# Seam order of weight splits and turned input, and weight halves in modulation steps, in a two-block transformer on one core

## The chip, the core and the metric

The kernel is one program on one NeuronCore of a Trainium2 chip. The metric is the device time of one execution in microseconds (us). Before the change three runs gave 1286.58, 1288.45 and 1289.17 us; their median is 1288.45 us. Engines are named as in the profile: PE is the matmul engine and PEld its weight load, DVE the vector engine, ACT the scalar engine, POOL the GpSimd engine, SP the engine whose queue issues the loads.

## The reference

Two blocks run one after the other on the same 256 tokens of width 1024, all in float32:

```
h = swiglu(rms_norm(x), ffn1_w_in, ffn1_w_out)          # 1024 -> 2 x 2816 -> 1024
x = x + 0.5 * rms_norm(h)
x = x + rms_norm(token_mixing(rms_norm(x)))              # retention + neighbourhood attention
x = x + 0.5 * rms_norm(swiglu(rms_norm(x), ffn2_w_in, ffn2_w_out))
mod = silu(c) @ ada_w + ada_b                            # 2 layers x 6 vectors of 1024
for i in (0, 1):                                         # moba attention, then differential attention
    shift1, scale1, gate1, shift2, scale2, gate2 = mod[i]
    y = attention_i(x * (1 + scale1) + shift1)
    x = layer_norm(sqrt(2) * x + (1 + gate1) * y)
    y = square(relu((x * (1 + scale2) + shift2) @ up)) @ down   # 1024 -> 4096 -> 1024
    x = layer_norm(sqrt(2) * x + (1 + gate2) * y)
```

What matters here is that 198 slots of 1 MB of weights and 48 MB of `ada_w` (the matrix of the modulation) are read once, and that each stage starts from a normalised, scaled and shifted copy of `x` with features on the partitions, which I call the turned input.

## The kernel before

The stages are, in order: ffn1, mixing, ffn2, attention 0, mlp 0, attention 1, mlp 1. A matmul in full float32 precision is made of three matmuls on operands of a reduced float32 type: a value `w` is split into a high part `wh` (rounded by a copy) and a low part `wl = w - wh`, and an input likewise; `mmA` and `mmB` issue high by high, high by low and low by high.

**The stream of weights.** `Stream` handles all weights in one fixed sequence of slots of 1 MB, each of two halves. A half is loaded to a `raw` tile (RAW = 6 of them, line 79 or 81, on SP's queue), ACT copies it to `wh` (line 115), and DVE subtracts to `wl` (line 93). One such step is `piece()`. The DVE part isn't issued at once: it goes to the list `late` and is issued by `flush(n)`, which leaves the newest `n` of the list. At most RING = 8 halves are held beyond the oldest one in use. Between the weights stand the halves of the modulation: a piece of `ada_w` is no weight but a multiply-add on DVE into `adacc` (line 339); after eight of them `ada_parts` (lines 345 to 358) cuts the sum into three bf16 parts by turns on ACT and DVE, and `spare` multiplies them by ones on PE (24 matmuls of one column, or three of 512 columns) when the next feed-forward step has room.

**What sets the order.** Every engine runs its instructions in the order in which this program issues them. PE's work is issued half by half, and after each half comes a `tick()`: it advances the stream (`Stream.tick`, line 135) by up to two pieces and then runs one turn of the background generators (the hidden activations, attention pairs, `ada_parts`). So what stands ahead of what on ACT and DVE is fixed by how many pieces a tick issues:

```
        for n in range(2):
            p = self.next_pos()
            if self.si >= len(self.seq) or p >= self.prog + look or 2 * p >= self.done + RING:
...
            mod = self.si not in self.wpos
            self.piece()
            if mod:
                break
```

`use(n, b)` (line 154) is called when PE's work for slot n is about to be issued; it makes the missing pieces and flushes the whole list.

**Seams.** A stage ends in `down_tail`: the four banks of the last product, by token half t and feature half f, are handed to `post.bank(t, f)`. `PostRms` (ffn1, mixing, ffn2) and `PostLn` (both attentions, mlp 0) normalise and add to `x`. Behind the last bank `ahead(3)` makes three pieces, and `flush(post.low)` keeps `low` splits back (2 for `PostRms`, 1 for `PostLn`). Then the next stage begins with `projT`: it calls `use` for its two slots and `turn(1)` for the second token half (the first was turned inside `down_tail`, by `mid`). `turn_of` (line 586) transposes eight 128 x 128 blocks on PE (tile `xt`). With a shift `c` given (the seams into attention and mlp) ACT scales and shifts them into `hf` (line 606), the high part goes to `XX` by a copy on ACT for t = 0 (line 612) and on DVE for t = 1 (line 610), and DVE subtracts the low part (line 613), in groups of 2, 2 and 4 blocks. Without a shift ACT writes the high part and DVE the low part straight from `xt` (lines 597, 598). PE's first matmul of the second half needs the first group.

Of the kernel before, what the change touches and what calls it, by code (L numbers as in the profile page):

```python
# [12 lines left out]
AF = mybir.ActivationFunctionType  # L13
# [35 lines left out]
class Stream:  # L49
# [39 lines left out]

    def flush(self, n=0):  # L90
        while len(self.late) > n:
            wl, raw, wh = self.late.popleft()
            self.nc.vector.tensor_tensor(wl, raw, wh.bitcast(F32), OP.subtract)  # L93

    def next_pos(self):
# [7 lines left out]
    def piece(self, lag=1):  # L103
        nc, i, h = self.nc, self.si, self.half
        raw = self.raw.pop((i, h))
        self.half += 1
        if self.half == 2:
            self.half, self.si = 0, i + 1
        if self.seq[i][0] == "w":
            n = self.wpos[i]  # L110
            assert 2 * n + h < self.done + RING, (n, h, self.done)
            wh = self.pool.tile([128, 1024], F32R, name="wh", bufs=RING)
            wl = self.pool.tile([128, 1024], F32R, name="wl", bufs=RING)
            self.parts[n, h] = (wh, wl)
            nc.scalar.activation(wh, raw, AF.Copy)  # L115
            self.late.append((wl, raw, wh))
            if lag is not None:
                self.flush(lag)
            self.load_to()
        else:  # L120
            self.flush()
            self.ada(self.seq[i][3], h, raw)
            self.load_to()
# [11 lines left out]
    def tick(self):  # L135
        self.prog += 0.5
        look = 1.5 if self.prog < 5 else LOOK
        for n in range(2):
            p = self.next_pos()
            if self.si >= len(self.seq) or p >= self.prog + look or 2 * p >= self.done + RING:  # L140
                if n == 0:
                    self.flush()
                    self.load_to()
                break
            mod = self.si not in self.wpos
            self.piece()
            if mod:
                break

    def ahead(self, n=1):  # L150
# [5 lines left out]
    def use(self, n, b):  # L156

        while self.next_pos() <= n + 0.5:
            self.piece()
        self.flush()  # L160
        return [[t.rearrange("p (k f) -> p k f", f=b) for t in self.parts[n, h]] for h in range(2)]

    def release(self, n, h):
# [8 lines left out]
def block_kernel(ctx, tc, A, out):  # L172
    nc = tc.nc
    V, SC, PE, GP = nc.vector, nc.scalar, nc.tensor, nc.gpsimd
# [14 lines left out]
    def w2(name, bufs=None):  # L189
        return work.tile([128, 512], F32, name=name, tag="w2", bufs=4)  # L190
# [135 lines left out]
    mod = const.tile([128, 96], F32, name="mod")  # L326
# [3 lines left out]
    def ada(key, h, w):  # L330
        l, s, i = key
        kb = 2 * i + h
        if kb == 0:
            ada_drain()
            adacc[0] = big.tile([128, D], F32, name="adacc")
            V.tensor_scalar(adacc[0], w, csil[:, 0:1], None, op0=OP.mult)
            return
        t = adacc[0]
        V.scalar_tensor_tensor(t, w, csil[:, kb:kb + 1], t, op0=OP.mult, op1=OP.add)  # L339
        if kb == 7:  # L340
            ada_now.append(ada_parts(l, s, t))
            start(ada_now[0], 1)
# [3 lines left out]
    def ada_parts(l, s, t):  # L346

        parts = [adap[-1].tile([128, D], BF16, name=f"ada{i}", bufs=1) for i in range(3)]
        SC.activation(parts[0], t, AF.Copy)
        yield 1  # L350
        V.tensor_tensor(t, t, parts[0], OP.subtract)
        yield 1
        SC.activation(parts[1], t, AF.Copy)
        yield 1
        V.tensor_tensor(parts[2], t, parts[1], OP.subtract)
        yield 1
        ada_now.clear()
        ada_out.append((l, s, parts, None if s in (2, 5) else 0))

# [92 lines left out]
    def proj(bank, then=nothing):  # L452

        n = nxt()
        for h, (wh, wl) in enumerate(st.use(n, 256)):
            for c in range(2):
                cs = slice(c * 128, (c + 1) * 128)
                for k in range(4):
                    mmB(two(bank)[:, c], wh[:, k, cs], wl[:, k, cs], XX[:, 4 * h + k],
                        h == 0 and c == 0 and k == 0, h == 1 and k == 3)  # L460
            st.release(n, h)
            if h:
                then()
            tick()

    def projv(bank, then=nothing):

        n = nxt()
        for h, (wh, wl) in enumerate(st.use(n, 256)):
            for t in range(2):  # L470
                for k in range(4):
                    mmA(two(bank)[:, t], wh[:, k], wl[:, k], XX[:, 4 * h + k, :, TS[t]],
                        h == 0 and t == 0 and k == 0, h == 1 and k == 3)
            st.release(n, h)
            if h:
                then()
            tick()

    def projA(banks, X, nk=KB, then=nothing):

        for i in range(nk // 4):
            n = nxt()
            for h, (wh, wl) in enumerate(st.use(n, 512)):
                for t in range(2):
                    for k in range(2):
                        kk = 4 * i + 2 * h + k
                        mmA(banks[t], wh[:, k], wl[:, k], X[:, kk, :, TS[t]], kk == 0, kk == nk - 1)
                st.release(n, h)
                if kk == nk - 1:
                    then()  # L490
                tick()
# [94 lines left out]
    def turn_of(src, a, c, alloc=gu):  # L586

        def turn(t):
            ps = [alloc("xt"), alloc("xt")]
            for k in range(8):  # L590
                PE.transpose(ps[k // 4][:, k % 4 * 128:k % 4 * 128 + 128], src[:, t, k * 128:(k + 1) * 128], ident)
            if c is None:
                for i in range(4):
                    for b in range(2):
                        k = 4 * b + i
                        x, h, l = ps[b][:, i * 128:(i + 1) * 128], XX[:, k, 0, TS[t]], XX[:, k, 1, TS[t]]
                        SC.activation(h, x, AF.Copy, scale=a[:, k:k + 1])
                        V.scalar_tensor_tensor(l, x, a[:, k:k + 1], h.bitcast(F32), op0=OP.mult, op1=OP.subtract)  # L598
                return
            for k0, n in ((0, 2), (2, 2), (4, 4)):  # L600
                if k0 != 2:
                    w = w2("hf").rearrange("p (k s) -> p k s", k=4)
                f = w[:, k0 % 4:k0 % 4 + n]
                for i in range(n):
                    k = k0 + i
                    SC.activation(f[:, i], ps[k // 4][:, k % 4 * 128:k % 4 * 128 + 128], AF.Identity,  # L606
                                  scale=a[:, k:k + 1], bias=c[:, k:k + 1])
                h, l = (XX[:, k0:k0 + n, i, TS[t]] for i in range(2))
                if t:
                    V.tensor_copy(h, f)  # L610
                else:
                    SC.activation(h, f, AF.Copy)
                V.tensor_tensor(l, f, h.bitcast(F32), OP.subtract)
        return turn

    class PostRms:

        low = 2
# [19 lines left out]

    class PostLn:

        low = 1

        def __init__(self, accs, gate):
            self.accs, self.gate = accs, gate
# [846 lines left out]
```

## Time and profile before

| what | value |
|---|---|
| median of three runs | 1288.45 us (1286.58 to 1289.17) |
| the profiled execution's own time | 1282.29 us |
| its span, first to last instruction | 1280.3 us |
| mean granted TensorE clock | 0.990 |
| PE busy | 1234.5 us, 96% of the span |
| DVE busy | 932.7 us, 73% |
| ACT busy | 642.5 us, 50% |
| loads | 269.37 MB, 211 GB/s over the span |

Busy time is the sum of the instructions' own durations where they do not overlap; matmuls are pipelined, so it is close to the span wherever PE is fed. The chain of waits (the work that ended last, followed back) gives PE 83% of the span, DVE 8%, ACT 3%. What the change can save therefore lies in the places where PE waits, which the view of waits sums up by the line that waits and the line that released it.

### The profile page before, as it was taken

How to read it: one execution, taken by the hardware profiler on the slowest of the kernel's cores; microseconds unless marked ns; L12 is line 12 of the kernel's file. 1: busy time of each engine (PE TensorE's matmuls, PEld its weight loads, DVE VectorE, ACT ScalarE, POOL GpSimd, SP SyncE). 2: the span in 40 equal slices, each digit the busy share in tenths (PEclk: the TensorE clock that was granted, in tenths of full speed). 3: DMA queues.
4: the chain of work that ended last, by engine and by line, in shares of the span. 5: the costliest groups of instructions: out<-in, count | busy, mean ns of one | idle time of the engine just before them, and what ended most of it. 6: DMA issues, size and time to landing. Idle time of an engine off the chain costs nothing.

```text
span 1280.3 us, 18974 instructions
## 1 busy us (share of the span) xinstructions
PE 1234.5 (96%) x7222; PEld 1066.3 (83%) x7222; DVE 932.7 (73%) x1295; ACT 642.5 (50%) x1038; POOL 37.8 (3%) x45
## 2 busy tenths in 40 slices
PE   9999989999999999999999998999998999899997
PEld 7888767888888878887889987999977887899995
DVE  5687866888667678768478668777868977775655
ACT  6553565546455455454456545444644555544440
POOL 0000000320000000000000000000000001000000
PEclk9999999999999999999999999999999999899999
DMA  9788778866566477888454346788765434576650
GB/s 314 259 274 281 236 269 184 251 214 185 196 226 214 148 249 265 287 281 283 147 173 130 126 132 197 254 289 286 263 207 168 129 116 148 179 243 220 230 198 34
DMA packets 167884, 271.68 MB, mean 212 GB/s; under 512 B 15888, under 2 KB 119664, under 8 KB 167792
## 3 DMA queue, kind: packets, MB, share of 16 engines
q1 hardware_dynamic: 161328, 268.36, 64.0%
q10 hardware_dynamic: 6464, 2.10, 1.0%
q8 instruction: 57, 0.93, 0.3%
q14 instruction: 35, 0.29, 0.1%
HBM read 269.37 MB, written 1.05 MB: 211 GB/s over the span
## 4 chain that ended last, share of the span: by engine, by line
PE 83%; DVE 8%; ACT 3%; issue 2%; DMA 2%; POOL 1%; SPq 0%; DVEq 0%; ACTq 0%; POOLq 0%
PE acc L201 22%; PE g L201 20%; PE u L201 14%; DVE wl L93 4%; PE q L201 3%; PE oacc L201 3%; PE k L201 3%; PE v L201 3%; PE yr L201 2%; PE as L201 2%; PE ao L201 1%; ACT hf L606 1%; PE nq L201 1%; PE nk L201 1%; PE rk L201 1%
## 5 line engine op out<-in xcount | busy, mean ns | idle before, releaser
L93 DVE TENSOR_TENSOR wl<-raw,wh 128x1024 fp32r<-128x1024 f32 x392 | 467.0, 1219 | 36.4 <-ACT wh L115 35.5
L115 ACT ACTIVATE wh<-raw 128x1024 fp32r<-128x1024 f32 x392 | 400.2, 1055 | 167.4 <-issue 27.7
L201 PE MATMUL acc<-wh,H 128*128 128x512 f32 x864 | 282.4, 395 | 3.0 <-ACT wh L115 3.0
L201 PE MATMUL g<-wh,XX 128*128 128x512 f32 x832 | 264.2, 392 | 1.6 <-DVE XX L598 1.5
L201 PEld LDWEIGHTS acc<-wh,H 128*128 128x128 f32 x864 | 163.1, 189 | 37.2 <-ACT wh L115 3.9
L201 PEld LDWEIGHTS g<-wh,XX 128*128 128x128 f32 x832 | 156.3, 188 | 35.4 <-DVE XX L598 2.0
L201 PE MATMUL acc<-wl,H 128*128 128x512 f32 x432 | 169.6, 393 | 1.7 <-DVE wl L93 1.7
L201 PE MATMUL g<-wl,XX 128*128 128x512 f32 x416 | 162.1, 390 | 0.8 <-DVE wl L93 0.8
L201 PE MATMUL u<-XX,wh 128*128 128x256 f32 x896 | 162.4, 283 | 0.0
L201 PEld LDWEIGHTS u<-XX,wh 128*128 128x128 f32 x896 | 141.4, 192 | 2.0
L201 PE MATMUL u<-XX,wl 128*128 128x256 f32 x448 | 126.8, 283 | 0.0
L339 DVE SCALAR_TENSOR_TENSOR adacc<-raw,csil,adacc 128x1024 f32<-128x1024 f32 x84 | 108.1, 1287 | 0.8
L201 PEld LDWEIGHTS acc<-wl,H 128*128 128x128 f32 x432 | 81.6, 189 | 18.4 <-DVE wl L93 3.1
L201 PEld LDWEIGHTS g<-wl,XX 128*128 128x128 f32 x416 | 78.2, 188 | 16.9 <-DVE wl L93 1.2
L201 PEld LDWEIGHTS u<-XX,wl 128*128 128x128 f32 x448 | 85.9, 192 | 0.0
L779 ACT ACTIVATE q<-u 128x512 f32<-128x512 f32 x28 | 16.7, 598 | 125.0 <-PE u L201 125.0
L780 DVE TENSOR_TENSOR q<-q,u 128x512 f32<-128x512 f32 x28 | 19.2, 687 | 74.0 <-ACT q L779 74.0
L716 ACT ACTIVATE a<-g,r 128x256 f32<-128x256 f32 x44 | 20.5, 473 | 93.9 <-PE g L201 93.9
L718 DVE SCALAR_TENSOR_TENSOR b<-g,r,a 128x256 f32<-128x256 f32 x44 | 20.9, 483 | 60.5 <-ACT a L716 60.5
L201 PE MATMUL v<-wh,XX 128*128 128x256 f32 (+1 forms) x192 | 48.4, 337 | 6.6 <-DVE XX L610 6.6
L201 PE MATMUL k<-XX,wh 128*128 128x256 f32 x256 | 47.3, 286 | 0.0
L201 PE MATMUL q<-XX,wh 128*128 128x256 f32 x256 | 47.2, 285 | 0.0
(288 smaller groups left out, 1761.6 us busy)
## 6 DMA issues: line engine op xcount, KB each, us to landing
raw<-in_ada_w_dram SPq DMA_DIRECT2D x96, 512.0 KB, 5.0
raw<-in_ffn_w_in_dram SPq DMA_DIRECT2D x176, 256.0 KB, 5.0
raw<-in_mlp_w_up_dram SPq DMA_DIRECT2D x64, 512.0 KB, 4.6
raw<-in_mlp_w_down_dram SPq DMA_DIRECT2D x64, 512.0 KB, 4.9
raw<-in_w_mix_in_dram SPq DMA_DIRECT2D x52, 512.0 KB, 4.9
raw<-in_ffn_w_out_dram SPq DMA_DIRECT2D x44, 512.0 KB, 5.6
raw<-in_moba_w_in_dram SPq DMA_DIRECT2D x24, 512.0 KB, 4.4
raw<-in_diff_w_in_dram SPq DMA_DIRECT2D x24, 512.0 KB, 4.6
```

The costliest lines, as they stand in the source:

```text
L93: self.nc.vector.tensor_tensor(wl, raw, wh.bitcast(F32), OP.subtract)
L115: nc.scalar.activation(wh, raw, AF.Copy)
L201: PE.matmul(o, l, r, start=start, stop=stop, skip_group_check=True)
L339: V.scalar_tensor_tensor(t, w, csil[:, kb:kb + 1], t, op0=OP.mult, op1=OP.add)
L606: SC.activation(f[:, i], ps[k // 4][:, k % 4 * 128:k % 4 * 128 + 128], AF.Identity, scale=a[:, k:k + 1], bias=c[:, k:k + 1])
L716: SC.activation(two(a)[:, t], ps[t][:, 0:256], AF.Silu, scale=r[0][:, t:t + 1])
L718: V.scalar_tensor_tensor(two(b)[:, t], ps[t][:, 256:512], r[0][:, t:t + 1], two(a)[:, t], op0=OP.mult, op1=OP.mult)
L779: SC.activation(q, p, AF.Relu)
L780: V.tensor_tensor(q, q, p, OP.mult)
```

## The change

Five edits to the order of issue; what is computed stays the same.

```diff
@@ Stream.tick
-        for n in range(2):
+        for n in range(3):
...
             mod = self.si not in self.wpos
             self.piece()
-            if mod:
+            if (mod or n == 1) and self.next_pos() >= self.prog + 1.5:
                 break
@@ Stream.use   (piece() and flush() carry the slot number n as a fourth entry of late)
-        self.flush()
+        while self.late and self.late[0][3] <= n:
+            self.flush(len(self.late) - 1)
@@ ada_parts
         V.tensor_tensor(parts[2], t, parts[1], OP.subtract)
-        yield 1
+        yield 2
         ada_now.clear()
@@ turn_of
-                if t:
-                    V.tensor_copy(h, f)
-                else:
-                    SC.activation(h, f, AF.Copy)
+                SC.activation(h, f, AF.Copy)
                 V.tensor_tensor(l, f, h.bitcast(F32), OP.subtract)
@@ PostLn
-        low = 1
+        low = 2
```

A tick may now issue up to three pieces, and goes on behind a piece of the modulation, or behind the second piece, if the next weight is less than 1.5 slots ahead of PE's place. `use` flushes only the splits of slots up to the one it was asked for. The part of the modulation is handed over one tick later. `turn(1)` copies the high part on ACT. `PostLn` keeps two splits back at the end, as `PostRms` does.

The first place is DVE at the seam from ffn2 into attention 0, from the last bank on (X is the residual, XX the turned input, hf its scaled and shifted form). Before:

```order
L633 TENSOR_SCALAR sa<-sa 128x1
L637 SCALAR_TENSOR_TENSOR X<-m,r,X 128x512 x2
L93 TENSOR_TENSOR wl<-raw,wh 128x1024 x3
L610 CAST XX<-hf 128x2x128
L613 TENSOR_TENSOR XX<-hf,XX 128x2x128
L610 CAST XX<-hf 128x2x128
L613 TENSOR_TENSOR XX<-hf,XX 128x2x128
L610 CAST XX<-hf 128x4x128
L613 TENSOR_TENSOR XX<-hf,XX 128x4x128
L93 TENSOR_TENSOR wl<-raw,wh 128x1024 x5
```

Now:

```order
L631 TENSOR_SCALAR sa<-sa 128x1
L635 SCALAR_TENSOR_TENSOR X<-m,r,X 128x512 x2
L93 TENSOR_TENSOR wl<-raw,wh 128x1024
L611 TENSOR_TENSOR XX<-hf,XX 128x2x128 x2
L611 TENSOR_TENSOR XX<-hf,XX 128x4x128
L93 TENSOR_TENSOR wl<-raw,wh 128x1024 x7
```

One split instead of three stands ahead of the turned input, the three copies are gone from DVE, and two splits more stand behind.

The second place is ACT in ffn1, in the ninth and tenth of its eleven steps (a is the gate's activation of a step, H the high part of its hidden tile). Before:

```order
L716 ACTIVATE a<-g,r 128x256 x2
L547 ACTIVATE H<-g 128x2x256
L115 ACTIVATE wh<-raw 128x1024 x4
L716 ACTIVATE a<-g,r 128x256 x2
L115 ACTIVATE wh<-raw 128x1024 x2
L547 ACTIVATE H<-g 128x2x256
```

Now:

```order
L714 ACTIVATE a<-g,r 128x256 x2
L115 ACTIVATE wh<-raw 128x1024 x2
L548 ACTIVATE H<-g 128x2x256
L115 ACTIVATE wh<-raw 128x1024 x3
L714 ACTIVATE a<-g,r 128x256 x2
L115 ACTIVATE wh<-raw 128x1024 x2
```

Between the two activations stand five high parts instead of four. Over the whole order up to the eighth and the tenth activation, ACT has made five and three halves more than before.

The third place is DVE in the tail of attention 0, at its first two banks (v is the sum that is normalised, bs its statistics). Before:

```order
L652 TENSOR_TENSOR v<-oacc,grow 128x512
L653 SCALAR_TENSOR_TENSOR v<-X,v 128x512
L654 BN_STATS bs<-v 128x6
L652 TENSOR_TENSOR v<-oacc,grow 128x512
L653 SCALAR_TENSOR_TENSOR v<-X,v 128x512
L654 BN_STATS bs<-v 128x6
L656 BN_AGGR mv<-bs 128x2
```

Now:

```order
L650 TENSOR_TENSOR v<-oacc,grow 128x512
L651 SCALAR_TENSOR_TENSOR v<-X,v 128x512
L652 BN_STATS bs<-v 128x6
L93 TENSOR_TENSOR wl<-raw,wh 128x1024
L650 TENSOR_TENSOR v<-oacc,grow 128x512
L651 SCALAR_TENSOR_TENSOR v<-X,v 128x512
L652 BN_STATS bs<-v 128x6
L654 BN_AGGR mv<-bs 128x2
```

One split that `use` issued ahead of the first bank now follows it, ahead of the second.

## Rows read from the trace of the kernel before

**Rows 1.** The page, part 1: busy us (share of the span) and instructions.
```profile
PE 1234.5 (96%) x7222; PEld 1066.3 (83%) x7222; DVE 932.7 (73%) x1295; ACT 642.5 (50%) x1038; POOL 37.8 (3%) x45
```

**Rows 2.** Waits: who waits <- for whom: us in total, times, longest us.
```profile
PE v L201 <- DVE XX L610: 6.6, 2, 3.6
PE u L201 <- DVE XX L610: 5.8, 2, 2.9
PE acc L201 <- ACT wh L115: 3.0, 2, 1.5
PE xt L591 <- DVE v L664: 2.9, 3, 1.3
PE g L201 <- DVE ada L355: 2.8, 3, 1.3
PE acc L201 <- DVE wl L93: 1.7, 3, 0.8
PE g L201 <- DVE XX L598: 1.5, 1, 1.5
PE g L724 <- DVE b L718: 1.0, 1, 1.0
PE rv L201 <- DVE XX L598: 0.8, 1, 0.8
```

**Rows 3.** The same view, ACT's wait for loads.
```profile
ACT wh L115 <- DMA raw<-in_ffn_w_in_dram: 24.2, 17, 3.9
```

**Rows 4.** Timeline of ACT in ffn1: start us, us, instructions [idle before <- releaser].
```profile
163.79 0.47 ACT L716 ACTIVATE a<-g,r 128x256 f32<-128x256 f32 x1 [8.61 <-PE g L201]
```

**Rows 5.** Timeline of DVE, ACT and PE at the seam into attention 0.
```profile
645.11 3.49 DVE L93 TENSOR_TENSOR wl<-raw,wh 128x1024 fp32r<-128x1024 f32 x3
648.51 0.29 DVE L610 CAST XX<-hf 128x256 fp32r<-128x256 f32 x1
...
637.22 0.81 ACT L606 ACTIVATE hf<-xt,mod,sc 128x128 f32<-128x128 f32 x2 [1.05 <-PE xt L591]
638.05 0.42 ACT L612 ACTIVATE XX<-hf 128x256 fp32r<-128x256 f32 x1
...
641.04 0.63 ACT L612 ACTIVATE XX<-hf 128x512 fp32r<-128x512 f32 x1
...
645.52 2.90 ACT L606 ACTIVATE hf<-xt,mod,sc 128x128 f32<-128x128 f32 x8 [0.43 <-PE xt L591]
...
648.85 0.50 PE L201 MATMUL v<-wh,XX 128*128 128x512 f32 x1 [2.93 <-DVE XX L610]
```

**Rows 6.** The chain that ended last, in order of time: start us, us, what.
```profile
605.97 4.44 PE acc L201 x12
...
648.85 5.72 PE v L201 x24
...
666.09 2.88 PE q L201 x24
...
774.36 10.00 PE u L201 x48
...
965.61 7.08 PE v L201 x24
...
1092.78 11.18 PE u L201 x48
```

**Rows 7.** Windows: us, busy (instructions) by engine, PEclk, DMA share, GB/s.
```profile
774.30:777.50 3.20, 3.14 (x8) 2.51 (x9) 3.10 (x7) 0.77 (x2) 0.00 (x0) 0.52 0.97 298
```

**Rows 8.** Timeline of DVE in the tail of attention 0.
```profile
756.65 0.69 DVE L652 TENSOR_TENSOR v<-oacc,grow 128x512 f32<-128x512 f32 x1 [0.57 <-PE oacc L201]
```

**Rows 9.** Timeline of DVE and PE in ffn2, one step with the modulation.
```profile
601.33 0.48 DVE L718 SCALAR_TENSOR_TENSOR b<-g,r,a 128x256 f32<-128x256 f32 x1 [0.88 <-ACT a L716]
...
603.34 0.60 PE L724 MATMUL g<-cst,b 128*128 128x128 f32 x4
```

**Rows 10.** Timeline of DVE at the seam into attention 1.
```profile
963.45 0.68 DVE L392 SCALAR_TENSOR_TENSOR grow<-adp,grow 128x512 f32<-128x512 f32 x1
```

More of the change, by code (lines that the diff above doesn't have):

```diff
@@ L91, in flush @@
         while len(self.late) > n:
-            wl, raw, wh = self.late.popleft()
+            wl, raw, wh, _ = self.late.popleft()
             self.nc.vector.tensor_tensor(wl, raw, wh.bitcast(F32), OP.subtract)
@@ L115, in piece @@
             nc.scalar.activation(wh, raw, AF.Copy)
-            self.late.append((wl, raw, wh))
+            self.late.append((wl, raw, wh, n))
             if lag is not None:
```

## The prediction, made before the changed kernel ran

> **What bounds the kernel now.** I read the page's busy shares first, then the waits of PE, then the timelines around the longest of them. PE is busy 1234.5 us [rows 1] of a span of 1280.3 us, so nearly all that can be saved lies in PE's waits, and in stretches where PE works at the lower of its two clock levels, 1.2 instead of 2.4 GHz. The waits [rows 2] come in three kinds. The largest are the seams: PE waits 6.6 and 5.8 us (two places each) for DVE's copy of the turned input into the two attentions and the two mlps, 1.5 us for its low part into ffn2 and 0.8 us into mixing. The second kind stands in ffn1: 3.0 us for two high parts of weights, and 1.7 us for low parts. The third is the modulation: 2.8 us for its last bf16 part. The reader is to see in the timeline of the seam [rows 5] why the first kind exists: DVE is free at 645.11, ACT has begun on the transposed blocks at 645.52, but DVE runs three splits of weights (3.49 us, 1.16 each) before its first copy at 648.51, and PE starts at 648.85 after 2.93 us. These splits belong to weights that PE needs only two slots later.
>
> **The change, part by part.** Times are those of the profiled execution.
>
> **A, tick.** At the two places in ffn1 PE waits for a high part that stands behind the gate's activation on ACT, which itself waits for PE: ACT had been idle for 8.61 us before it [rows 4]. So the order made these halves late, not the engine. By the new order ACT has made five and three halves more by then, and PE's next two halves are among them. The waits for high parts, 3.0 us, and two of the three for low parts, some 1.5 of 1.7 us [rows 2], go: 4.5 us. What covers the earlier pieces is that idle time of ACT; where it is gone, the loads are late next: ACT waits 24.2 us in all for ffn1 and ffn2 loads [rows 3]. Bounds: 0, if these loads are the true cause, and 4.7. I take 4.5, since the rows name ACT's order and not a load. In ffn2 and mlp 0 the same edit only moves pieces ahead; no weight is waited for there, and I cost it at nothing.
>
> **B, one tick more for the modulation.** PE's two waits of 1.3 us [rows 2] for the last bf16 part go, 2.6 us, since PE meets the products of the modulation one half of weights, some 2.7 us, later. Behind the second, twelve matmuls took 4.44 us [rows 6]; at the seam into attention 0 twenty-four such took 5.72, so twelve are 2.86 at most: 1.6 us lost to the lower clock, and gained. Together 4.2 us; bounds 1.3 and 4.4.
>
> **C and D, seams without a shift.** Into mixing the 0.8 us [rows 2] goes. Into ffn2 the 1.5 us goes, but two splits more then stand on DVE ahead of the gated product for which PE already waits 1.0 us (g <- b) [rows 2]; I take back 0.4 us and keep 1.1. Bounds for the two: 0.8 + 0.5 and 0.8 + 1.5.
>
> **E, into attention 0.** One split is left: DVE is free at 645.11 + 1.16 = 646.27. The copies are on ACT now, and the first token half shows that pattern [rows 5]: the scaling begins at 637.22, the copy of the first group ends 1.25 us later, that of the last 4.45 us later. From 645.52 this gives a first group at 646.77, when PE can start, 2.0 us before 648.85. The last group is ready at 649.97; PE, at 0.68 us a block (5.72 us for eight blocks [rows 6]), wants it at 649.6, and its low part a little later still: 0.5 us is given back. Gain 1.5 us; bounds 1.0 and 2.0. The two splits moved behind the turned input are wanted only after the projection of values, over 5 us later.
>
> Moving a copy from DVE to ACT is itself a loss by the rows: 128 x 256 takes 0.29 us there and 0.42 us here [rows 5]. The Trainium skill, ScalarE: Activation LUTs, section Rules for kernel authors, advises VectorE over ScalarE for simple elementwise work, and VectorE: DVE Perf Modes, section The perf-mode tier table, gives a float32 copy twice the rate of a two-tensor operation; the rows agree with both (0.29 against 0.42 us). By that rule the copies should have stayed, and the seam would give 2.0 instead of 1.5 us, four times over 2 us more. The sum keeps the 1.5: the two splits of 1.16 us that leave DVE outweigh what the copies cost.
>
> **F and H, into mlp 0 and mlp 1.** The same 1.5 us, less a new delay: a split of 1.16 us now stands between the first two banks of the tail, where DVE had 0.57 us to spare [rows 8], so the normalised first half, its transposes and everything chained behind come up to 0.6 us later; I take 0.5. Each 1.0 us; bounds 0.4 and 2.0.
>
> **G, into attention 1.** Here DVE also ran an operation of 0.68 us on the gate's row [rows 10] between the splits. It is now in the mlp's steps, so the seam loses 2 x 1.16 + 0.68 = 3.0 us of DVE, of which ACT's own chain lets PE have 2.7, less 0.5 for the last group; but three matmuls of 512 columns (0.24 us each by 5.72 / 24), which ran while PE waited anyway, now cost 0.7 us elsewhere. Gain 1.5 us; bounds 0.7 and 2.5.
>
> **I, the clock behind the seams.** Behind F, G and H PE worked at the lower level: granted clock 0.52 from 774.3 to 777.5 [rows 7], after some 4.2 us of waiting in two pieces (xt <- v and u <- XX [rows 2]). Against the seam into attention 0, which waits 2.93 us and keeps its clock, the loss is 7.08 - 5.72 = 1.4 us into attention 1, and, with 5.72 for the seam's own matmuls, 2.88 for the next twenty-four and 0.2 between, 10.00 - 8.8 = 1.2 and 11.18 - 8.8 = 2.4 us into the mlps [rows 6]: 5.0 us. The new waits are shorter than 2.93 us each, but still in two pieces, so I take 3.5, nearer to what the seam without loss shows; bounds 0 and 5.0.
>
> **Sum:** 4.5 + 4.2 + 0.8 + 1.1 + 1.5 + 1.0 + 1.5 + 1.0 + 3.5 = 19.1 us, so the profiled execution's 1282.29 us becomes 1263.2. The median of the runs is 1288.45, 6.2 us above that execution; with the same saving it becomes 1269.4 us.
>
> **Rivals.** *The clock still falls* at the seams and behind the modulation. For it: three pieces of waiting remain. Against it: they add up to less than the single wait that kept the clock. Without I and B's 1.6 the saving is 14.0 us: 1274.5 us. Chance 0.17. *The loads are the cause in ffn1*: earlier pieces ask for loads that come no sooner, and ACT waits for them in front of the activation. For it the 24.2 us [rows 3], against it the releasers in rows 2. Without A the saving is 14.6 us: 1273.9 us. Chance 0.12. *The waits only change place*: splits put behind the seams and halves put ahead in the steps make the hidden activations late, and A, C, D and I come to nothing while the rest is halved, about 5 us less the new waits: within 2.6 us of before, 1287 us. Chance 0.08. *Slower*, by the extra halves: in a step of ffn1 or ffn2 the gated product ends at 601.81 and PE transposes it at 603.34 [rows 9], 1.5 us of room. One more split of 1.16 us ahead of it is hidden; two, 2.3 us, cost 0.8 us a step, three cost 2.0. At three in each of twenty steps 40 us are lost against 19 gained: 1309 us. It decides from the second extra split that DVE reaches after the gate's activation. Against it: DVE waits for that activation already [rows 9], with nothing queued, so extra splits run before it. Chance 0.05. That the edit of tick does nothing is excluded by the new order on ACT; in mixing, the attentions and mlp 1 it does move almost nothing.
>
> **How the numbers follow.** The forecast has the rest, 0.58, and with the two rivals on its side (0.17 and 0.12) it is faster by over 0.2%, 2.6 us, which is about what a measurement of this kernel can tell from no change: 0.87. Within 0.2%: 0.08. Slower: 0.05. The upper bounds of A to I add up to 25 us, and the low end takes them: 1263 us. The high end covers both first rivals together (saving 9.5 us, 1279) and low bounds of some seams: 1283 us. Outside lie the case of no change and the slower one, 0.13, and little more.
>
> **What would show it.** In the changed profile DVE shows one split between the update of X and the first XX at every seam; PE's wait for the turned input falls below 1.5 us at each of the four seams, and is released by ACT or by DVE's line 611, not by a copy; the two waits for wh in ffn1 and those for ada are gone; the clock shows no stretch near 0.52 behind the seams. I am wrong if PE waits in ffn1 are released by loads, if PE waits for b in the feed-forward steps, or if the seams' waits come back as waits for v before the transposes.

## The result, and the profile after

The changed kernel takes 1275.71 us (median of seven runs, 1269.08 to 1279.27) against 1285.59 us (seven runs, 1281.79 to 1289.17): a ratio of 0.992, interval 0.9903 to 0.9937, or some 10 us. The direction was right and the time lies in the range, but the saving is about half of the 19.1 us that were summed. The forecast of 1269.4 us started from 1288.45, the median of the first three runs of the kernel before; from the 1285.59 of all seven the same sum gives 1266.5. The profiled execution took 1275.26 us with a span of 1273.5 us, 6.8 us less than that of before.

First the page of the changed kernel, part 1, which answers to [rows 1].

```profile
PE 1237.0 (97%) x7216; PEld 1067.3 (84%) x7222; DVE 928.7 (73%) x1283; ACT 651.7 (51%) x1050; POOL 38.4 (3%) x45
```

PE's idle time fell from 1280.3 - 1234.5 = 45.8 us to 1273.5 - 1237.0 = 36.5 us, but its busy time rose by 2.5 us. Where the waits went stands in the view of waits of the changed kernel, which answers to [rows 2, 3].

```profile
PE xt L592 <- DVE v L662: 5.0, 6, 1.3
PE g L722 <- DVE b L716: 3.9, 2, 3.7
...
PE u L202 <- DVE ada L356: 2.9, 2, 2.0
PE v L202 <- ACT XX L610: 2.0, 3, 0.9
...
PE u L202 <- ACT XX L610: 1.8, 2, 0.9
...
PE g L202 <- DVE ada L356: 1.3, 1, 1.3
...
PE acc L202 <- DVE wl L93: 0.2, 1, 0.2
...
ACT wh L115 <- DMA raw<-in_ffn_w_in_dram: 34.5, 17, 5.1
```

Gone are the waits for wh in ffn1 (3.0 us) and nearly all for wl (1.7 to 0.2), and at the four shifted seams 12.4 us of waiting for the turned input became 3.8 us, released by ACT. Three waits are larger than before: for v ahead of the transposes (2.9 to 5.0 us, six places instead of three), for the modulation (2.8 to 4.2) and for the gated product b (1.0 to 3.9). ACT waits longer for ffn loads than before (24.2 to 34.5 us), but no PE wait in ffn1 stands behind it.

The timelines of DVE, ACT and PE at the seam into attention 0 answer to [rows 5].

```profile
640.45 1.22 DVE L93 TENSOR_TENSOR wl<-raw,wh 128x1024 fp32r<-128x1024 f32 x1
642.13 0.43 DVE L611 TENSOR_TENSOR XX<-hf,XX 128x256 fp32r<-128x256 f32 x1 [0.47 <-ACT XX L610]
...
640.85 0.81 ACT L607 ACTIVATE hf<-xt,mod,sc 128x128 f32<-128x128 f32 x2 [0.42 <-PE xt L592]
641.68 0.42 ACT L610 ACTIVATE XX<-hf 128x256 fp32r<-128x256 f32 x1
...
644.68 0.63 ACT L610 ACTIVATE XX<-hf 128x512 fp32r<-128x512 f32 x1
...
642.15 0.50 PE L202 MATMUL v<-wh,XX 128*128 128x512 f32 x1 [0.91 <-ACT XX L610]
...
645.36 0.50 PE L202 MATMUL v<-wh,XX 128*128 128x512 f32 x1 [0.20 <-ACT XX L610]
...
648.49 0.40 PE L202 MATMUL q<-XX,wh 128*128 128x256 f32 x2
```

One split stands ahead, and PE waits 0.91 us where it waited 2.93. But ACT begins the copy of the last group 3.0 us behind that of the first, so PE's 24 matmuls take 648.49 - 642.15 = 6.34 us from start to start, against 5.57 (648.85 to the same matmul at 654.42) before. The seam gains 2.0 and gives back 0.8.

At the other three shifted seams the clock still fell; the windows behind them, and behind two places in ffn1 and ffn2, have the columns of [rows 7].

```profile
642.10:648.50 6.40, 6.15 (x25) 4.39 (x26) 4.01 (x6) 6.34 (x13) 0.00 (x0) 1.00 0.28 85
...
766.90:770.10 3.20, 3.19 (x8) 2.53 (x9) 0.85 (x3) 3.14 (x9) 0.00 (x0) 0.51 0.54 164
961.10:964.50 3.40, 3.40 (x10) 2.63 (x10) 1.19 (x3) 3.34 (x8) 0.00 (x0) 0.51 0.54 159
1087.40:1090.80 3.40, 3.40 (x9) 2.73 (x9) 1.15 (x3) 3.34 (x8) 0.00 (x0) 0.51 0.50 154
459.70:462.90 3.20, 3.20 (x10) 2.54 (x9) 3.20 (x4) 1.35 (x2) 0.00 (x0) 0.51 0.73 243
135.10:138.50 3.40, 3.40 (x10) 2.62 (x9) 3.40 (x5) 0.80 (x1) 0.00 (x0) 0.51 0.90 314
```

The clock of 0.51 is the level of 1.2 GHz. Ahead of these three seams' stretches PE waits 1.23 to 1.31 us for v, turns eight blocks, and waits 0.9 us; at the seam into attention 0 it goes into the eight blocks without a wait, waits 0.91 us behind them and keeps 2.4 GHz.

**The new wait in ffn2.** It is the largest single one, 3.73 us, at the first gated product. Timelines of SP's queue, DVE, ACT and PE of the changed kernel:

```profile
443.39 8.19 SPq L79 DMA_DIRECT2D raw<-in_ffn_w_in_dram  x4
...
449.33 0.16 DVE L697 SCALAR_TENSOR_TENSOR s<-s 128x2 f32<-128x2 f32 x1 [2.52 <-ACT junk L585]
449.41 6.90 DVE L93 TENSOR_TENSOR wl<-raw,wh 128x1024 fp32r<-128x1024 f32 x6
...
455.46 1.06 ACT L115 ACTIVATE wh<-raw 128x1024 fp32r<-128x1024 f32 x1 [2.37 <-DMA raw<-in_ffn_w_in_dram]
456.54 1.28 ACT L714 ACT_TABLE_LOAD   x1
457.83 0.84 ACT L714 ACTIVATE a<-g,r 128x256 f32<-128x256 f32 x2
...
458.34 0.87 DVE L716 SCALAR_TENSOR_TENSOR b<-g,r,a 128x256 f32<-128x256 f32 x2 [2.03 <-ACT a L714]
...
458.88 1.21 PE L722 MATMUL g<-cst,b 128*128 128x128 f32 x4 [3.73 <-DVE b L716]
```

The same two places in the kernel before:

```profile
446.75 3.49 DVE L93 TENSOR_TENSOR wl<-raw,wh 128x1024 fp32r<-128x1024 f32 x3
...
447.99 2.02 SPq L79 DMA_DIRECT2D raw<-in_ffn_w_in_dram  x4
```

The two splits that `use` no longer flushes stand on DVE behind the operation on `s`, which waits 2.52 us for ACT's squares. Until a split is done its `raw` tile is held, so the four loads queued for these tiles take 8.19 us to issue where they took 2.02. ACT's next wh then waits 2.37 us for its load, with the gate's activation behind it on ACT's queue, and b and PE follow.

### The profile page after: what moved, and what is told of

Same layout as the page of the kernel before. It is cut to its first block, busy times and chain, and to the rows that moved or that the text cites. A ratio compares the mean times of both kernels' runs of the same rounds, so it can differ in the third digit from the quotient of the medians.

```text
span 1273.5 us, 18976 instructions
## 1 busy us (share of the span) xinstructions
PE 1237.0 (97%) x7216; PEld 1067.3 (84%) x7222; DVE 928.7 (73%) x1283; ACT 651.7 (51%) x1050; POOL 38.4 (3%) x45
```

## The experiments

Each run's ratio is to the kernel before, timed beside it. Stage lengths are differences of the starts of PE's transposes in each profile: a stage counts from those of the second token half at its entry (ffn1 from the last four of x) to those of the first half at its end. Start-up is left out, since the transposes of x came anywhere from 10.8 to 13.9 us between kernels that begin alike.

**Old tick (e1_old_tick).**

```diff
-        for n in range(3):
+        for n in range(2):
...
-            if (mod or n == 1) and self.next_pos() >= self.prog + 1.5:
+            if mod:
```

> The change without its edit of tick (two pieces at most, none behind a piece of the modulation). Theory: the edit of tick is what ended ffn1's waits, so the two waits of acc for wh (1.5 us each) and for wl (0.8 us each) come back and the stretch from the first matmuls of ffn1 to its seam is 4 to 6 us longer than with the whole change (183.7 us there, 189.1 before); mlp 0, which the whole change made 3.1 us longer, gives back 2 to 3 us, since there the edit pulled the modulation ahead. In all 1 to 4 us slower than the whole change. Rival: the shorter ffn1 comes from the handing over of the modulation and from keeping splits back in use; then ffn1 stays within 1 us of 183.7.

Measured: 1273.26 us, ratio 0.9898 (0.987 to 0.9927). The waits in ffn1 are back, as the view of waits of this kernel shows:

```profile
PE g L722 <- DVE b L716: 3.6, 1, 3.6
PE acc L202 <- ACT wh L115: 3.0, 2, 1.5
...
PE acc L202 <- DVE wl L93: 1.7, 3, 0.8
```

ffn1 takes 188.5 instead of 183.7 us: the edit is worth 4.8 us there. But mlp 0 takes 180.2 instead of 183.9 and attention 1 114.3 instead of 116.6, and no wait for ada is left in mlp 0, so the whole is not the 1 to 4 us slower that were expected: the edit costs outside ffn1 what it gives there. PE waits for ada nowhere in this kernel. At the seam into attention 1 DVE's operation on the gate's row (line 393 here) stands ahead again, and PE waits 1.2 us for it: the edit of tick is what had moved it. The wait for b is not its doing.

**Tick in ffn1 alone (e6_tick_ffn1).**

```diff
-        for n in range(3):
+        for n in range(3 if self.prog < 33 else 2):
...
-            if (mod or n == 1) and self.next_pos() >= self.prog + 1.5:
+            if (mod or n == 1) and (self.prog >= 33 or self.next_pos() >= self.prog + 1.5):
```

> The change with its edit of tick in ffn1 alone; from ffn2 on a tick is as before. Theory: the edit pays only where weights were late, in ffn1 (4.8 us by the run that undid it), and costs 3.7 us in mlp 0 by pulling the modulation ahead of its hand-over; so ffn1 stays within 1 us of 183.7 us, mlp 0 falls to 180 to 181 us, ffn2 to 188 to 189 us, and the whole is 4 to 6 us shorter than with the change. Rival: what mlp 0 gained in that run came from the place of the modulation after a slower ffn1, and it stays at 183 to 184 us here.

Measured: 1268.16 us, ratio 0.9869 (0.985 to 0.9889). ffn1 stays at 183.7 us and mlp 0 falls to 180.0. The timelines of DVE and PE in mlp 0 show why; first the changed kernel:

```profile
815.29 4.62 DVE L93 TENSOR_TENSOR wl<-raw,wh 128x1024 fp32r<-128x1024 f32 x4
819.83 1.22 DVE L352 TENSOR_TENSOR adacc<-adacc,ada 128x1024 f32<-128x1024 f32 x1
...
822.25 2.35 DVE L93 TENSOR_TENSOR wl<-raw,wh 128x1024 fp32r<-128x1024 f32 x2
824.52 1.22 DVE L356 TENSOR_TENSOR ada<-adacc,ada 128x1024 bf16<-128x1024 f32 x1
...
823.57 0.20 PE L202 MATMUL u<-small,ada 128*128 128x1 bf16 x2
825.79 0.70 PE L202 MATMUL u<-small,ada 128*128 128x1 bf16 x22 [2.02 <-DVE ada L356]
```

And the tick in ffn1 alone:

```profile
822.32 0.69 DVE L778 TENSOR_TENSOR q<-q,u 128x512 f32<-128x512 f32 x1 [3.77 <-ACT q L777]
...
830.34 1.22 DVE L356 TENSOR_TENSOR ada<-adacc,ada 128x1024 bf16<-128x1024 f32 x1
...
835.46 0.75 PE L202 MATMUL u<-small,ada 128*128 128x1 bf16 x24
```

With two pieces a tick DVE waits 3.77 us for ACT, and the last part of the modulation ends 3.9 us ahead of PE. With three, four splits stand ahead of its first subtraction and two ahead of the second, and PE waits 2.02 us. Yet the last part does not come later than it did. Counted from the start of mlp 0 (764.93 us in the change, 765.60 here) DVE ends it at 60.8 us in the change and at 66.0 here, and PE begins its products at 58.6 and at 69.9. The third piece pulls the modulation's own pieces ahead as well, so that PE's products fall into an earlier step of the mlp, 11.2 us sooner, and DVE, with the splits in its queue, is only 5.2 us sooner. In ffn1, where the edit stays, it is the same: PE meets the second modulation 116.6 us into the stage and waits 1.4 us, where the kernel before met it at 136.5 and did not wait.

**Old hand-over (e2_old_hand).**

```diff
-        yield 2
+        yield 1
```

> The change with the modulation's last part handed over after one tick again instead of two. Theory: PE meets the products of the modulation before DVE has reached the last part, because splits stand ahead of it on DVE; a tick is about 2.7 us of PE's work, so taking one away adds up to 2.7 us at each place that waits already (ffn1 1.3, mlp 0 2.0 and 0.9 us) and makes others wait: the waits for ada rise from 4.2 us to 8 to 14 us, and the time by as much as 4 to 10 us. Rival: the number of ticks doesn't matter, since the products go into the next feed-forward step in any case; then the waits stay within 1 us of 4.2.

Measured: 1284.44 us, ratio 0.9988 (0.9967 to 1.0009). Waits of PE for the modulation in this kernel:

```profile
PE u L202 <- DVE ada L356: 4.9, 3, 2.2
...
PE u L202 <- ACT ada L354: 3.9, 2, 3.1
...
PE g L202 <- DVE ada L356: 1.9, 1, 1.9
```

These are 10.7 us of waits instead of 4.2, and mlp 0 takes 194.0 us. Without the later hand-over the extra pieces eat all that the change gives.

**Seams only (e10_seams_only)**: the old tick and the old hand-over together, by the two diffs above.

> The changed kernel with both the old tick and the old hand-over of the modulation, so that only the four edits at the seams are left (splits only up to the slot used, copies on ACT, two splits kept). Theory: the hand-over one tick later is worth 2 to 4 us beside the old tick (term B) and far more beside the new one (9 us were measured there), so this kernel lies 1 to 5 us above the one with the old tick alone (ratio to the kernel before 0.991 to 0.995), PE's waits for ada come back to 2 to 4 us, ffn1 keeps its waits for wh (3.0 us) and the seams keep theirs as in the change. Rival: beside the old tick the hand-over is worth nothing, and the seams carry the whole gain: ratio 0.989 to 0.990.

Measured: 1277.5 us, ratio 0.994 (0.9919 to 0.9961). Against the old tick alone (0.9898) the hand-over is worth 5.4 us, though the two intervals just overlap, and the seams alone some 7 us. The waits for ada are 2.8 us as in [rows 2], those for wh 3.0. PE waits 3.8 us for b here too, so the wait in ffn2 comes from the seam. The two kernels also show how the hand-over works at the two places where PE waits for ada here: PE meets the third modulation of ffn1 176.1 us into the stage here and at 190.7 with the old tick alone, the last one of ffn2 at 159.0 and at 175.4. The products move on to the next place that takes them, some 15 us, and not by one half of weights.

**Hand-over two ticks later (e5_hand3).**

```diff
-        yield 2
+        yield 3
```

> The change with the modulation's last part handed over after three ticks. Theory: in the changed order DVE reaches that part 1.0 to 2.2 us after PE wants it; one tick more is about 2.7 us of PE's work, so the three waits for it that are left (1.3, 2.0, 0.9 us) go and mlp 0 is 3 to 4 us shorter than with the change (183.9 us from seam to seam there), and the whole 3 to 6 us shorter, with the lower clock behind ffn1's wait. Rival: the products only land on another place where DVE is late too, and the waits stay above 2.5 us in sum.

Measured: 1274.68 us, ratio 0.9916 (0.9901 to 0.993): the same as the change. The waits for ada are 3.5 us (1.8 and 1.7) instead of 4.2; the 3 to 6 us expected did not come. In mlp 0 PE meets the products 58.6 us into the stage with one, two or three ticks alike, and the last part ends at 64.2, 60.8 and 59.7 us: the third tick brings it only 1.1 us nearer.

**Splits ahead of the squares (e4_flush_sq).** One line at the seams into mixing and ffn2, behind `turn(1)` and ahead of the squares:

```diff
+                    st.flush()
```

> The change with one addition: at the seams into mixing and ffn2 the two kept splits are issued directly behind the turned input, ahead of the squares' sum for which DVE waits 2.5 us for ACT. Theory: the kept splits hold their raw tiles over that wait, so loads start late, ACT waits 2.4 us for one of them and PE 3.7 us for the first gated product of ffn2 (1.0 before the change). With the splits ahead of the sum PE's wait there falls to 0 to 1.2 us, the lower clock behind it goes, and the time falls by 3 to 5 us. Rival: the gated product is late because of DVE's and ACT's own work up to it, whatever the order; then the wait stays above 2.5 us.

Measured: 1272.42 us, ratio 0.9887 (0.9858 to 0.9916). Timelines of SP's queue, DVE and PE of this kernel:

```profile
444.27 5.49 SPq L79 DMA_DIRECT2D raw<-in_ffn_w_in_dram  x4
...
447.59 2.35 DVE L93 TENSOR_TENSOR wl<-raw,wh 128x1024 fp32r<-128x1024 f32 x2
450.20 0.16 DVE L697 SCALAR_TENSOR_TENSOR s<-s 128x2 f32<-128x2 f32 x1 [0.26 <-ACT junk L585]
...
457.27 0.94 PE L722 MATMUL g<-cst,b 128*128 128x128 f32 x4 [1.21 <-DVE b L716]
```

The two splits fit into DVE's wait, the loads issue in 5.49 us, that wait for b falls to 1.21 us (a second one, of 1.19 us, appears in a later step) and ffn2 from 189.3 to 186.6 us. That is the mechanism read above, undone by one line. For the whole time the interval overlaps that of the change.

**Copies on DVE (e3_dve_copy).**

```diff
-                SC.activation(h, f, AF.Copy)
+                if t:
+                    V.tensor_copy(h, f)
+                else:
+                    SC.activation(h, f, AF.Copy)
```

> The change with the high part of the second token half copied on DVE again (line 610 of before), all else as changed. Theory: with one split ahead DVE is free when ACT has scaled the first group, and ACT alone then sets the pace with 0.36 us a block instead of 0.55; the waits for the turned input (3.8 us for copies on ACT over four seams) fall to 2 to 3 us and the second and third groups no longer wait, in all 1 to 2.5 us less than the whole change. Rival: DVE, which then does copy and subtraction, is the slower of the two; the low part comes later and the four seams are 0 to 2 us longer.

Measured: 1272.39 us, ratio 0.9882 (0.9845 to 0.9918). PE at the seam into mlp 0 of this kernel, and the windows behind the last three seams, all at the upper level:

```profile
764.01 0.50 PE L202 MATMUL u<-wh,XX 128*128 128x512 f32 x1 [0.77 <-DVE XX L611]
...
763.90:767.10 3.20, 3.09 (x13) 2.48 (x14) 2.46 (x7) 3.20 (x8) 0.00 (x0) 1.00 0.56 164
958.50:961.90 3.40, 3.40 (x15) 2.74 (x16) 2.69 (x6) 3.40 (x7) 0.00 (x0) 1.00 0.55 157
1084.40:1087.80 3.40, 3.39 (x15) 2.73 (x16) 2.69 (x6) 3.40 (x7) 0.00 (x0) 1.00 0.48 154
```

PE waits 0.1 us less ahead of the seam, and its 24 matmuls take 5.6 us at every seam instead of 6.3 (attention 0) to 7.2: the first 0.8 of this is ACT's chain, the rest the clock. The four seams together take 34.9 us from the start of the last matmul ahead of the transposes to the start of the first one behind the 24, in the change 40.8 and before 48.6. At the seam into attention 0, where the clock holds in all three kernels, it is 7.6, 8.5 and 9.8 us. Once a single split stands ahead, DVE is free in time, and the copy there is the shorter way. The whole time fell by some 5 us against the change by the ratios, but the two intervals overlap. The Trainium skill's advice on simple elementwise work (ScalarE: Activation LUTs, Rules for kernel authors; its row names relu, max, min, add and mul), which the prediction weighed and set aside, holds here for a copy too.

**Idle matmuls at the seams (e7_fill)**: 16 matmuls of 128 columns ahead of the second half's transposes and 14 behind them, at the four shifted seams, on a bank whose content is not used.

```diff
+            if t:
+                warm(banks[1], fill[0])
...
+            if t:
+                warm(banks[1], fill[1])
...
-                projT(bs, turn, copy)
+                projT(bs, turn, copy, (16, 14))
```

> The change with idle matmuls of 128 columns at the four seams with a shift, on a bank that the next product overwrites: 16 ahead of the transposes of the second token half and 14 behind them. Theory: the lower clock behind three of these seams comes from the two waits (1.4 and 1.1 us) around the transposes; filled with matmuls of about 0.055 us each they leave the clock at 1.0, the 24 matmuls behind each seam take 5.8 us instead of 7, and the time falls by 2 to 4 us, though the fill itself adds up to 0.3 us a seam. Rival: the clock falls for another reason (what DVE and ACT do, or the transposes themselves), stays at 0.5 behind two or three of the seams, and the time stays or rises by up to 1.5 us.

Measured: 1274.93 us, ratio 0.992 (0.9903 to 0.9936). The granted clock is 1.00 in the 3.4 us behind each of the three seams, and the four seams take 39.3 us instead of 40.8; with the splits ahead of the squares, where the clock held without added matmuls, they take 38.4. So the added matmuls take back some 0.9 of the 2.4 us. The whole time is that of the change, as mlp 0 takes 185.5 us instead of 183.9 with a fall of the clock behind its wait for ada. It proves little of the clock, since kernels without them (splits ahead of the squares, hand-over two ticks later) kept theirs as well.

**Splits at the start of the tail (e11_tail_flush).** One line at the start of `down_tail`:

```diff
+        st.flush()
```

> The changed kernel with one line more: all splits held back are issued at the start of the tail of each stage, ahead of its first bank. Theory: the split that stands between the first two banks delays the normalised first half, so that PE waits for v before the first transposes six times; with it issued ahead, PE's waits for v (5.0 us over 6) fall to about 3 us over 3, and the time falls by 1 to 3 us (ratio 0.989 to 0.991). Rival: DVE reaches the first bank late anyway, the split ahead of it delays it as much, and the waits stay at 4 us or more: same time.

Measured: 1274.96 us, ratio 0.9929 (0.9911 to 0.9948). PE's waits for v are 3.9 us over three places instead of 5.0 over six: the three ahead of the first half's transposes are gone. But the time did not fall by the 1 to 3 us expected: in this profile the wait for b in ffn2 is 5.4 us (4.2 the longest). The cause is shown, its worth here is not.

**All joined (e12_best_no_flush, e9_best1)**: the tick in ffn1 alone, the copies on DVE and the splits ahead of the squares; and the same with the splits at the start of the tail.

> The kernel that joins the tick in ffn1 alone, the copies on DVE and the splits ahead of the squares, without the splits issued at the start of the tail. Theory: this kernel is 1 to 3 us slower than the one with them (which had 0.982 of the kernel before), so a ratio of 0.983 to 0.985, with PE waiting for v six times again. Rival: with the old tick outside ffn1 nothing is held back there, and the ratio stays at 0.982.

> Four corrections together on the change: its edit of tick in ffn1 alone, the copy of the second half's high part on DVE, the two kept splits ahead of the squares' sum at the seams into mixing and ffn2, and all splits issued at the start of a stage's tail, so that none stands between the tail's first two banks. Theory: the single parts gave, in stretches, 0.5 to 1 us a seam for the copy, 2.7 us in ffn2, about 3.7 in mlp 0, and the last should give back 0.5 us a seam before the transposes (waits of xt for v, 5.0 us in sum, to 3.0 us): 9 to 12 us less than the change, 1.6 to 1.8% under the kernel before. Rival: the parts share the same idle time of DVE and the sum is under 6 us.

Measured: 1264.4 us, ratio 0.9844 (0.9826 to 0.9862), and 1262.26 us, ratio 0.9819 (0.9797 to 0.9841). Both beat the kernel before and the change; the last is 23 us below before, more than the 19.1 that were summed. The 3 us between the two are not certain, as the intervals overlap. Waits of the last one, for v at three places only, for the modulation once and for b once:

```profile
PE xt L593 <- DVE v L666: 3.6, 3, 1.3
...
PE g L202 <- DVE ada L356: 1.3, 1, 1.3
PE g L726 <- DVE b L720: 1.2, 1, 1.2
```

## Why the prediction was right and wrong, by its steps

| term | predicted us | measured us |
|---|---|---|
| A, in ffn1 | 4.5 | 4.8 (old tick against the change) |
| A, elsewhere | 0 | a loss of 4 (stages) to 7 (ratios), by the tick in ffn1 alone |
| B | 4.2 | 5.4 beside the old tick; beside the new one PE's waits for ada are 4.2 where they were 2.8 before |
| C | 0.8 | 0.8 (mixing 228.6 to 227.8, seams only) |
| D | 1.1 | a loss of 0.9 (ffn2 189.4 to 190.2, seams only) |
| E to H with I | 8.5 | 7.8 at the seams, all of it in PE's waits, less 1.2 ahead of the first half's transposes |

**A** was right where its rows were: ACT's order made the halves late, and the rival of the loads is refuted, since no load releases a PE wait in ffn1. The step that failed is "in ffn2 and mlp 0 the same edit only moves pieces ahead; no weight is waited for there, and I cost it at nothing". Among the pieces moved ahead are the modulation's own. PE then meets their products a step sooner (11.2 us in mlp 0), and DVE, which ends the modulation and has 1.2 us more to do for every piece, is only 5.2 us sooner. The edit costs 3.8 us in mlp 0, 2.9 of them in two waits for ada.

**B** by itself did more than it promised: beside the old tick no wait for ada is left. Its step was mis-sized, since the products move on by some 15 us, and not by the 2.7 us of one half of weights. But what B moves back, A pulls ahead; here the later hand-over only pays for the extra pieces. A and B had been summed as if each stood alone.

**D** failed in its mechanism. I took back 0.4 us for two splits of DVE ahead of b. What costs is what the kept splits hold: their `raw` tiles, and so the next loads. PE's wait for b grew by 2.7 us.

**E to H**: the waits of 2.9 and 3.6 us fell to 0.9, as E's chain said (2.0 us earlier). The late last group cost 0.8 us instead of the 0.5 taken: 6.34 us for the 24 matmuls at the seam into attention 0, and 6.33 to 6.35 at all four seams with the splits ahead of the squares, where the clock held. (The 0.68 us a block of E is a slip: 5.72 us for eight blocks is 0.715, and the 649.6 goes with that.) The first half's transposes now wait some 0.4 us at three tails, not two; the split between the first two banks is the cause, since the waits go with it. The pair of 0.29 and 0.42 us that the prediction gives for its two citations compares a copy on DVE with one on ACT and says nothing of a copy against a two-tensor operation. For that, at the same seam of the kernel before, DVE's copies of 256 and 512 columns take 0.29 and 0.42 us and its subtractions 0.42 and 0.69: 0.13 against 0.27 us for the added 256 columns, but not half for a whole operation.

**I** did not come in the profiled execution: the clock fell at all three seams again. The step "they add up to less than the single wait that kept the clock" failed as an argument: 1.31 + 0.91 us is less than 2.93, and the clock fell. Each fall cost less, 0.7 to 0.9 us by 7.0 to 7.2 us for the 24 matmuls against 6.34, where they had cost 1.4, 1.4 and 2.6, since ACT's late last group already holds PE back at the upper level. But that group took as much: the 24 matmuls of the four seams together take 27.7 us, and before 27.6.

The timed runs look better. Their mean granted clock rose from 0.988 (median of 27 executions of the kernel before, timed beside the experiments) to 0.992 (median of the six executions of the change beside the profiled one). Over those 27 executions 0.001 more of it goes with a time some 1.0 us shorter (a straight line through them), so the rise stands for some 4 us; this is an estimate, of the size of I and the clock's part of B together (5.1 us). The two profiled executions, 0.990 and 0.989, do not show it. By this estimate some 4 of the 10 us won are clock, and of the 14 us of waits only 6 (by the timed runs) to 8 (by the profiles) came.

Of the rivals, *the clock still falls* names 1274.5 us, close to the 1275.7 measured; but A's loss and D's are not in it, so that closeness is luck. *The waits only change place* describes ffn2 and mlp 0. The slow rival asked for two extra splits ahead of b in each step; the wait for b came once, and by the loads. Of the signs named in advance, one split ahead of the turned input, waits for it below 1.5 us at each seam and the end of the waits for wh came. The waits for ada did not go, and three stretches near 0.51 stand behind the seams. Of the three signs of being wrong two came in part: PE waits for b in ffn2, and its waits for v rose from 2.9 to 5.0 us. So the direction is right by the mechanism at the seams and in ffn1; that the time lies in the range is owed to its high end, which left room for lost terms.

**Open**: why the clock falls at a seam in one profile and not in the next. Of the last three seams it fell at three in the change, at two with the old tick, at one each with the tick in ffn1 alone, with the old hand-over, with the seams only and with the splits at the start of the tail, and at none with the splits ahead of the squares or the hand-over two ticks later, though PE's wait behind the transposes is the same 0.9 us in nearly all. With the copies on DVE it fell at one of nine seams in three kernels, so shorter waits seem to help; that is a tendency in single profiles and no more. Of the 2.4 us in attention 1 between the old tick and the change, 1.1 us lie in the seam; the rest was not taken apart.

## What to carry to other kernels

Work put ahead into an engine's idle time is free only if nothing with a due time comes along: when a step issues more, list what else it moves, who asks for that sooner, and whether every engine that makes it is as much sooner, not only the one that was idle. A delayed operation keeps its source buffer, so moving it back moves the next load back too; put it into a wait that the engine has anyway, as the splits ahead of the squares were. And two edits that use the same slack are not to be summed.

## What the runs showed that was not expected

Holding two buffers a few microseconds longer made four issues take 8.19 us instead of 2.02, and one PE wait 3.73 us out of it. Two waits of PE of 1.3 and 0.9 us with eight transposes between them were followed by 3.4 us at the lower clock in some kernels' profiled executions and not in others, while a single wait of 2.93 us kept the clock. Pieces issued sooner made a result come 5.2 us sooner and PE wait 2.0 us longer for it, because PE asked for it 11.2 us sooner. And a fall of the clock costs less where PE is fed slowly anyway: 0.7 to 0.9 us against 1.4.
